# Activation tiles moved by 64 bytes, the convolution's tap blocks on VectorE, and a new order of its steps

## The chip, the cores and the metric

The kernel runs on one core of a Trainium2 chip. The metric is the device time of one execution in microseconds (us), as the median of several runs. Engines are named as the profile names them: PE (TensorE's matmuls), PEld (TensorE's weight loads), DVE (VectorE), ACT (ScalarE), POOL (GpSimd) and SP (SyncE, which issues DMAs).

## The reference

The input is 256 positions of 1,024 channels in float32. Two transformer layers and a third block follow one another; each needs the result of the one before.

```python
def first_block(...):
    for layer in range(2):
        mix = even_mixer(...) if layer % 2 == 0 else odd_mixer(...)
        h = h + mix
        h = h + swiglu(rmsnorm(h, g_ffn[layer]), w_gate[layer], w_up[layer], w_down[layer])
        gate = sigmoid(rmsnorm(h, g_ple[layer]) @ w_ple_gate[layer])
        h = h + gate * (p[layer] @ w_ple_proj[layer])

def conformer_conv(h, w_in, b_in, w_dw, b_dw, ln_g, ln_b, w_out):
    a, gt = split(h @ w_in + b_in)
    u = a * sigmoid(gt)
    y = depthwise_causal_conv31(u, w_dw) + b_dw
    return silu(layernorm(y, ln_g, ln_b)) @ w_out

def second_block(x, c, ...):
    x = x + g1 * conformer_conv(rmsnorm_2(x, g) * (1 + sc1) + sh1, ...)
    x = x + g2 * hier_moe(rmsnorm_2(x, g) * (1 + sc2) + sh2, ...)
    return rmsnorm_2(x, final_g)
```

The mixers are a short gated convolution with spatial gating (layer 0) and an attention with a chunked recurrence (layer 1). `hier_moe` sends each position to 2 of 32 experts. The change acts on all the dense products and on `conformer_conv`, whose depthwise convolution has 31 taps.

## The kernel before, in words

**Dense products.** A weight comes from HBM in pieces of 128x2048 into `raw` (`load`, line 153, issued by SP). `prep` (line 160) splits a piece into two tiles of the type fp32r in one slot `hl`: ACT copies the high part (line 66 is the helper that records it), DVE subtracts it to get the low part (line 70). Activations are split in the same way: `xTh` and `xTl` hold the transposed input, high and low; `aTh`/`aTl`, `yTh`/`yTl` and others hold those of other products. A product is three matmuls (`mm3`, line 118, or `passes`, line 1286), high by high, high by low and low by high, all recorded at line 111. In nearly all of them the activation is the stationary operand (128x128, loaded by PEld) and the weights stream past it, 512 columns at a time. In the convolution's input product (the steps named i below) it is the other way round: `hl` is stationary and 256 columns of `xTh` or `xTl` stream.

**Addresses.** `shift_by(pool, n)` (line 34) allocates a gap of n bytes per partition, so that all tiles behind it in the pool move. Before, the gap ahead of `xTh` is 64 bytes. In the built program `xTh` then stands at byte 12192 of each partition, which is 160 modulo 256, and so do `xTl` and the other split activations; each slot of `hl` is 224 modulo 256. The activations stand 64 bytes below the weights, modulo 256.

**The conformer convolution.** The 1,024 channels are eight tiles m = 0 to 7 of 128. The first three tiles' input products are made for each half h of the positions, with the activations stationary, the others by `conv_in_proj(m)`, 48 matmuls of 256 columns each. `conv_u(m)` (line 1180) makes the gated tile u: ACT takes the tanh, DVE multiplies (line 79). Tile 0 is convolved on DVE, tap by tap (`yc<-u,wtap,yc`, line 79, one 128x256 instruction for a tap), drained in the background while PE goes on. Tiles 1 to 7 are convolved on PE: POOL's queue writes u to `ud` in HBM (line 1197), the closure `back` has SP read it again in another layout, four DMAs into `u4` (line 1202, three buffers), and `conv_pe(m)` (line 1262) runs 64 matmuls of 256 columns (line 1266) whose stationary operands are the tap blocks `taps[m]`. A tap block is a 128x1024 product of the filter `wcv` with the identity, made by `conv_taps_w(m)` (line 1174), on POOL before (`e=G`); there are four buffers (`TAPS`), so the block of tile m+4 is made behind `conv_pe(m)`. The first four are issued ahead of the products of tiles 0 to 2 (line 1289).

**The order.** The program is scheduled by hand: instructions run on each engine in the order in which the code issues them, and DMAs queue on SP in the same way. The loop at line 1426 follows a string, `TG["plan"]` (line 1919): iM is `conv_in_proj(M)`, cM is `conv_pe(M)`, r issues the reads waiting in `reads` except the last, a issues all of them, s is `conv_pivot` (a mean over two tiles that the other tiles are shifted by), R and t prepare the router's weights (`r_start`, line 1333, begins with an iota on POOL and three small DVE operations), p preps a weight of the next product. Each matmul counted by `mm` may also release background work.

**After it** come the layer norm, the output product, the router, and the experts' stage, in which weights of 1 MB each are read from HBM, in fp32 and used once.

Of the kernel before, what the change touches and what calls it, by code (L numbers as in the profile page):

```python
# [11 lines left out]
I32 = mybir.dt.int32  # L12
# [11 lines left out]
FAR = 1024.0  # L24
# [9 lines left out]
def shift_by(pool, n):  # L34

    gaps.append(n)
    pool.tile([128, n // 4], F32, name=f"gap{len(gaps)}", tag=f"gap{len(gaps)}")
# [3 lines left out]
def kernel(ctx, tc, A, out, stop=None):  # L41
    nc = tc.nc
    V, S, T, G, SP = nc.vector, nc.scalar, nc.tensor, nc.gpsimd, nc.sync
# [7 lines left out]
    xp = ctx.enter_context(tc.tile_pool(name="xp", bufs=1))  # L51
# [3 lines left out]
    dconst = dense_stack.enter_context(tc.tile_pool(name="dconst", bufs=1, side="right"))  # L55
    small = dense_stack.enter_context(tc.tile_pool(name="small", bufs=2, side="right", reuse_waits="tile"))
# [7 lines left out]
    def act(o, i, f, scale=1.0, bias=0.0, accum_out=None):  # L64
        if accum_out is None:
            return S.activation(o, i, f, bias=bias, scale=scale)  # L66
        return S.activation(o, i, f, bias=bias, scale=scale, accum_out=accum_out)  # L67

    def tt(o, a, b, op, e=None):
        return (e or V).tensor_tensor(o, a, b, op=op)  # L70

    def ts(o, a, s1, s2, op0, op1=None, e=None):
        if op1 is None:
            return (e or V).tensor_scalar(o, a, s1, None, op0=op0)  # L74
        return (e or V).tensor_scalar(o, a, s1, s2, op0=op0, op1=op1)
# [6 lines left out]
    def red(o, i, op):  # L82
        return V.tensor_reduce(o, i, op=op, axis=AX.X)

    MUL, ADD, SUB, MAX, MIN = ALU.mult, ALU.add, ALU.subtract, ALU.max, ALU.min
# [101 lines left out]
    def nxt(kept=False):  # L187
        i = at_[1]
        at_[1] += 1
        if kept:  # L190
            hold.append(first_half[i])
        return lambda k: need(i, k)


    X = xp.tile([128, 2, D], F32, name="X")
    shift_by(xp, 64)
    xTh = xp.tile([128, 2, 8, 128], F32R, name="xTh", tag="xTh")
    xTl = xp.tile([128, 2, 8, 128], F32R, name="xTl", tag="xTl")

# [5 lines left out]
                    base=0, channel_multiplier=-1)  # L205
# [7 lines left out]
                    base=0, channel_multiplier=-1)  # L213
# [3 lines left out]
                    base=0, channel_multiplier=-1)  # L217
    ones = const.tile([128, 128], F32, name="ones")
    G.memset(ones, 1.0)

    col, ncol = col_plan()
    vc = dconst.tile([128, ncol], F32, name="vc")
# [883 lines left out]
    eye = dconst.tile([128, 32], F32, name="eye")  # L1106
# [13 lines left out]
    def preload(n):  # L1120
        while len(moe_w) < min(n, 6 * NEXP):
            q = len(moe_w)
            pair, r = divmod(q, 12)
            s_ = q % SLOTS
            if s_ < EARLY:
                t_ = early.tile([128, 2048], F32, name="ew", tag="ew")
            elif s_ < EARLY + NEXT:
                t_ = nexts.tile([128, 2048], F32, name="nw", tag="nw")
            elif s_ < EARLY + NEXT + RING:
                t_ = ring.tile([128, 2048], F32, name="raw", tag="raw")  # L1130
            elif s_ < EARLY + NEXT + RING + WRING:
                t_ = wring.tile([128, 2048], F32, name="wr", tag="wr")
            else:
                t_ = split.tile([128, 2048], F32, name="hl", tag="hl")
            if q < 6 * NEXP - 2:
                SP.dma_start(t_, A["moe"][2 * pair + r % 2, r // 2])
            moe_w.append(t_)
            if q == 6 * NEXP - 1:
                for c in range(2):
                    for e in range(2):  # L1140
                        sl = slice(1024 * c, 1024 * c + 1024)
                        SP.dma_start(moe_w[q - 1 + e][:, sl], A["moe"][2 * pair + e, 5, :, sl])
# [9 lines left out]
    iota64 = rt.tile([128, 64], F32, name="iota64")  # L1152
    iom = rt.tile([128, 32], F32, name="iom")
# [2 lines left out]
    gate = rt.tile([128, 2, 32], F32, name="gate")  # L1156
    rank = rt.tile([128, 2, 32], F32, name="rank")
    cnt = rt.tile([128, 32], F32, name="cnt")
    cstk = ExitStack()
    cp = cstk.enter_context(tc.tile_pool(name="conv", bufs=1, side="right", reuse_waits="tile"))  # L1160
    ustk = ExitStack()
# [10 lines left out]
    taps, u4, reads = {}, {}, []  # L1172

    def conv_taps_w(m):

        taps[m] = cu.tile([128, 32, 32], F32, name="taps", tag="taps", bufs=TAPS)
        tt(taps[m], wsh[:, m, :, None].to_broadcast([128, 32, 32]),
           eye[:, None, :].to_broadcast([128, 32, 32]), MUL, e=G)

    def conv_u(m, pt):  # L1180
        sg = cu.tile([128, 256], F32, name="sg", tag="sg", bufs=2)
# [80 lines left out]
    def conv_pe(m):  # L1262
        pt = psum("mm")
        for i in range(8):
            for g in range(4):
                T.matmul(pt[32 * g:32 * g + 32, 0:256], taps[m][:, 8 * g + i, :],
                         u4[m][:, g, 4 * i:4 * i + 256], start=i == 0, stop=i == 7)
            if background:
                background.pop(0)[1]()
        if m in PIVOT:  # L1270
            act(yc[:, m, :], pt[:, 0:256], AF.Identity, bias=vc[:, c0 + m:c0 + m + 1])
        else:
            stt(yc[:, m, :], pt[:, 0:256], vc[:, c0 + m:c0 + m + 1], shift, ADD, SUB)
            conv_sums(m)

    def conv_pivot():

        pt = psum("aux")
        for m in PIVOT:
            T.matmul(pt[:, 0:256], ones, yc[:, m, :], start=m == PIVOT[0], stop=m == PIVOT[-1])  # L1280
        ts(shift, pt[:, 0:256], 1.0 / 256, None, MUL)
        shifted[0] = True
        for m in list(PIVOT) + unshifted:
            conv_shift(m)
# [1 line left out]
    def passes(wk):  # L1286
        return ((wk[0], xTh), (wk[0], xTl), (wk[1], xTh))

    for m in range(ONDVE, ONDVE + TAPS):
        conv_taps_w(m)  # L1290
    first_w = [nxt(True) for _ in range(3)]
    pm = [psum("mm") for _ in range(3)]
    um, us = {}, {}
# [22 lines left out]
    def conv_in_proj(m):  # L1316
        w = nxt(True)
        pt = psum("mm")
        for c in range(2):
            o = pt[:, 256 * c:256 * c + 256].rearrange("p (h t) -> p h t", h=2)  # L1320
            for k in range(8):
                for i, (w_, x_) in enumerate(passes(w(k))):
                    mm(o, w_[:, c * 128:(c + 1) * 128], x_[:, :, k, :], k == 0 and i == 0, k == 7 and i == 2)
        hold.clear()
        conv_u(m, pt)
# [4 lines left out]
    def rtile(name, *shape, pool=None):  # L1330
        return (pool or rt).tile([128] + list(shape), F32, name=name)

    def r_start():

        iota_i = small.tile([128, 512], I32, name="iota_i", tag="xf")[:, 0:64]
        G.iota(iota_i, pattern=[[1, 64]], base=0, channel_multiplier=0)
        V.tensor_copy(iota64, iota_i)
        ts(iom, iota64[:, 0:32], -64.0, None, ADD)
        ts(iota64, iota64, -FAR, None, ADD)
        wr = vc[:, col["w_r"]:col["w_r"] + 288].rearrange("p (k n) -> p k n", k=8)  # L1340
        gs = small.tile([128, 512], F32, name="gs", tag="xf")[:, 0:288].rearrange("p (k n) -> p k n", k=8)
        tt(gs, wr, modc[:, 24:32, None].to_broadcast([128, 8, 36]), MUL)
        shw = rtile("shw", 36, pool=cp)
        red(shw, gs.rearrange("p k n -> p n k"), ADD)
        gw = wr
        tt(gw, wr, moe_g[:, :, None].to_broadcast([128, 8, 36]), MUL)
        router.extend([gw, shw])

    def r_shift():
        pt = psum("aux")  # L1350
        T.matmul(pt[:, 0:36], ones, router[1], start=True, stop=True)
        rc = rtile("rc", 36, pool=cp)
        tt(rc, pt[:, 0:36], row("b_r"), ADD)
        router[1] = rc
# [60 lines left out]
    def r_rank():  # L1415
# [6 lines left out]
        stt(rank, asg, -FAR, rp[:, 0:64].rearrange("p (h e) -> p h e", h=2), MUL, ADD)  # L1422
        act(cnt, rp[:, 64:96], AF.Copy)

    bg_every[0] = TG["bg"][1]
    for step in TG["plan"].split():
        m = int(step[1:] or 0)
        if step[0] == "i":
            conv_in_proj(m)
        elif step in "ra":  # L1430
            while len(reads) > (step == "r"):
                reads.pop(0)()
        elif step == "o":
            preload(len(moe_w) + 1)
        elif step[0] == "c":
            conv_pe(m)
            if m + TAPS < 8:
                conv_taps_w(m + TAPS)
        elif step == "s":
            conv_pivot()  # L1440
        elif step == "R":
            r_start()
        elif step == "t":
            r_shift()
        elif step == "p" and at_[0] < len(halves):
            prep()
# [403 lines left out]
    R, frow = end[2], end[1]  # L1850
# [32 lines left out]
def bass_f32(x, bits=24):  # L1883
# [7 lines left out]
ONDVE = 1  # L1891
LN_AHEAD = 5
TAPS = 4
# [26 lines left out]
}  # L1920
PIVOT = (1, 2)
K8 = ((0, 4), (4, 4))
# [58 lines left out]
def col_plan():  # L1981
    return offsets(COLS, lambda o, n: o)
# [74 lines left out]
```

## Time and profile before

| what | value |
|---|---|
| median of 3 runs | 1265.97 us (1257.66 to 1267.45) |
| the profiled execution: its time, and its span | 1260.12 us, 1258.3 us |
| PE busy | 1191.8 us, 95% of the span |
| PEld busy | 817.2 us, 65% |
| DVE, ACT, POOL busy | 647.2 us (51%), 482.9 us (38%), 76.3 us (6%) |
| moved by DMA | 361.87 MB, mean 288 GB/s |
| mean granted TensorE clock | 0.992 |

The span is the stretch of the profiled execution that the trace covers; 1.8 us of that execution's time lie around it. A busy PE is not PE at its peak, since matmuls are pipelined and their recorded lengths overlap; the distance from one start to the next, called the pitch here, says what a matmul costs in a row of them. A granted clock of 1.00 is 2.4 GHz, 0.50 is 1.2 GHz.

### The profile page before, as it was taken

How to read it: one execution, taken by the hardware profiler on the slowest of the kernel's cores; microseconds unless marked ns; L12 is line 12 of the kernel's file. 1: busy time of each engine (PE TensorE's matmuls, PEld its weight loads, DVE VectorE, ACT ScalarE, POOL GpSimd, SP SyncE). 2: the span in 40 equal slices, each digit the busy share in tenths (PEclk: the TensorE clock that was granted, in tenths of full speed). 3: DMA queues.
4: the chain of work that ended last, by engine and by line, in shares of the span. 5: the costliest groups of instructions: out<-in, count | busy, mean ns of one | idle time of the engine just before them, and what ended most of it. 6: DMA issues, size and time to landing. Idle time of an engine off the chain costs nothing. (4 is left out here: it accounts for less than half of the span.)

```text
span 1258.3 us, 15805 instructions
## 1 busy us (share of the span) xinstructions
PE 1191.8 (95%) x6143; PEld 817.2 (65%) x6143; DVE 647.2 (51%) x1079; ACT 482.9 (38%) x802; POOL 76.3 (6%) x109
## 2 busy tenths in 40 slices
PE   7999999999889999999998899999999999898995
PEld 5888888888777788888887777444444444343432
DVE  6767677677767688775465865522112221111114
ACT  7545544446875474444364433311101111110111
POOL 1100000001030000000004140000000000000000
PEclk9999999999999999999999999999999999999999
DMA  9654777874533189765644759699999999999992
GB/s 332 237 168 184 263 279 269 285 300 140 183 136 130 38 325 374 270 236 196 216 135 182 228 182 393 259 421 421 420 420 421 420 421 419 422 420 421 421 419 100
DMA packets 60716, 361.87 MB, mean 288 GB/s; under 512 B 7296, under 2 KB 11040, under 8 KB 22496
## 3 DMA queue, kind: packets, MB, share of 16 engines
q1 hardware_dynamic: 59184, 357.27, 73.5%
q0 software_dynamic: 1024, 3.05, 0.8%
q8 instruction: 49, 0.80, 0.3%
q10 hardware_dynamic: 432, 0.53, 0.1%
q14 instruction: 27, 0.22, 0.1%
HBM read 358.71 MB, written 2.11 MB: 287 GB/s over the span
## 5 line engine op out<-in xcount | busy, mean ns | idle before, releaser
L111 PE MATMUL mm<-hl,xTh 128*128 128x512 f32 (+3 forms) x1376 | 423.9, 388 | 12.4 <-ACT hl L66 6.0
L70 DVE TENSOR_TENSOR hl<-raw,hl 128x1024 fp32r<-128x1024 f32 (+3 forms) x240 | 284.7, 1217 | 94.0 <-ACT hl L66 90.6
L111 PEld LDWEIGHTS mm<-hl,xTh 128*128 128x128 f32 x1376 | 256.0, 190 | 64.2 <-ACT hl L66 6.4
L66 ACT ACTIVATE hl<-raw 128x1024 fp32r<-128x1024 f32 (+3 forms) x240 | 240.7, 1032 | 136.9 <-PE mm L111 102.1
L111 PE MATMUL mm<-hl,xTl 128*128 128x512 f32 (+3 forms) x688 | 265.5, 386 | 2.7 <-DVE xTl L70 2.7
L111 PEld LDWEIGHTS mm<-hl,xTl 128*128 128x128 f32 x688 | 130.7, 190 | 28.2 <-DVE xTl L70 3.8
L111 PE MATMUL mm<-hl,aTh 128*128 128x512 f32 x352 | 109.7, 392 | 0.0
L1625 PE MATMUL gu<-hl,xg 128*64 128x512 f32 x392 | 101.6, 603 | 5.9 <-DMA hl<-in_moe_dram 5.9
L70 DVE TENSOR_TENSOR hid<-gu,hid 128x512 f32<-128x512 f32 x16 | 11.1, 692 | 184.4 <-PE gu L1625 184.4
L1625 PEld LDWEIGHTS gu<-hl,xg 128*64 128x64 f32 x392 | 35.3, 139 | 62.4 <-issue 51.2
L111 PEld LDWEIGHTS mm<-hl,aTh 128*128 128x128 f32 x352 | 66.1, 188 | 13.8
L79 DVE SCALAR_TENSOR_TENSOR yhl<-w,gc,yhl 128x512 fp32r<-128x512 f32 x30 | 22.5, 751 | 97.3 <-ACT yhl L66 95.4
L111 PE MATMUL mm<-hl,aTl 128*128 128x512 f32 x176 | 69.3, 394 | 0.0
L1625 PE MATMUL gu<-wr,xg 128*64 128x512 f32 x216 | 63.1, 595 | 5.5 <-DMA wr<-in_moe_dram 5.5
L80 DVE SCALAR_TENSOR_TENSOR ada<-ada,crow 128x1024 f32<-128x1024 f32 x48 | 58.4, 1220 | 7.3 <-DMA ada<-in_ada_dram 7.3
L66 ACT ACTIVATE yhl<-w,gc 128x512 fp32r<-128x512 f32 x30 | 20.6, 687 | 106.1 <-PE w L1650 106.1
L66 ACT ACTIVATE xg<-w,modc,moe_g 128x256 f32<-128x256 f32 x32 | 18.1, 564 | 85.3 <-PE w L1596 85.3
L1650 PE MATMUL w<-hl,hid 128*64 128x512 f32 x184 | 47.6, 597 | 3.3 <-DVE ogT L74 3.3
L66 ACT ACTIVATE hid<-gu 128x512 f32<-128x512 f32 x16 | 9.6, 597 | 102.0 <-PE gu L1625 102.0
L1625 PE MATMUL gu<-raw,xg 128*64 128x512 f32 x152 | 44.5, 593 | 0.9 <-DMA raw<-in_moe_dram 0.9
L1625 PE MATMUL gu<-ew,xg 128*64 128x512 f32 x152 | 43.7, 594 | 0.4 <-DMA ew<-in_moe_dram 0.4
L1625 PEld LDWEIGHTS gu<-wr,xg 128*64 128x64 f32 x216 | 20.6, 137 | 36.1 <-issue 25.1
(453 smaller groups left out, 1494.8 us busy)
## 6 DMA issues: line engine op xcount, KB each, us to landing
raw<-in_dense_dram SPq DMA_DIRECT2D x108, 1024.0 KB, 5.2
hl<-in_moe_dram SPq DMA_DIRECT2D x72, 1024.0 KB, 19.8
wr<-in_moe_dram SPq DMA_DIRECT2D x45, 1024.0 KB, 19.8
ew<-in_moe_dram SPq DMA_DIRECT2D x28, 1024.0 KB, 19.9
raw<-in_moe_dram SPq DMA_DIRECT2D x27, 1024.0 KB, 19.8
ada<-in_ada_dram SPq DMA_DIRECT2D x48, 512.0 KB, 7.7
nw<-in_moe_dram SPq DMA_DIRECT2D x18, 1024.0 KB, 19.8
raw<-in_dense_dram SPq DMA_DIRECT2D x8, 512.0 KB, 6.9
```

Source lines behind the costliest of these rows:

```text
L66: return S.activation(o, i, f, bias=bias, scale=scale)
L70: return (e or V).tensor_tensor(o, a, b, op=op)
L79: return V.scalar_tensor_tensor(o, a, s, b, op0=op0, op1=op1)
L80: return V.scalar_tensor_tensor(o, a, s, b, op0=op0, op1=op1, accum_out=accum_out)
L111: T.matmul(o, lhsT, rhs, start=start, stop=stop_)
L1625: T.matmul(o[64 * e:64 * e + 64, :], xg[:, k, s0 + 64 * e:s0 + 64 * e + 64], ws[e][:, kk * 512:(kk + 1) * 512], start=k == 0, stop=k == 7)
L1650: T.matmul(py[c][64 * e:64 * e + 64, :], hT[:, k, 64 * e:64 * e + 64], ws[e][:, (2 * c + kk) * 512:(2 * c + kk + 1) * 512], start=k == 0, ...
```

## The change

It has four parts. (1) The gap ahead of `xTh` grows from 64 to 128 bytes: `xTh` stands at byte 12256, 224 modulo 256, like the slots of `hl`, and the other split activations move with it to the same residue. (2) DVE makes the tap blocks instead of POOL, and the first four are issued behind the products of tiles 0 to 2, ahead of the plan. (3) The plan changes: each r now issues exactly one read, and the steps c come later among the steps i. (4) The router's iota moves to the start of the kernel, and its three small DVE operations ahead of the convolution.

```diff
-    shift_by(xp, 64)
+    shift_by(xp, 128)
...
+    iota_i = dconst.tile([128, 64], I32, name="iota_i")
+    G.iota(iota_i, pattern=[[1, 64]], base=0, channel_multiplier=0)
...
+    V.tensor_copy(iota64, iota_i)
+    ts(iom, iota64[:, 0:32], -64.0, None, ADD)
+    ts(iota64, iota64, -FAR, None, ADD)
...
         taps[m] = cu.tile([128, 32, 32], F32, name="taps", tag="taps", bufs=TAPS)
         tt(taps[m], wsh[:, m, :, None].to_broadcast([128, 32, 32]),
-           eye[:, None, :].to_broadcast([128, 32, 32]), MUL, e=G)
+           eye[:, None, :].to_broadcast([128, 32, 32]), MUL)
...
-    for m in range(ONDVE, ONDVE + TAPS):
-        conv_taps_w(m)
     first_w = [nxt(True) for _ in range(3)]
...
-        iota_i = small.tile([128, 512], I32, name="iota_i", tag="xf")[:, 0:64]
-        G.iota(iota_i, pattern=[[1, 64]], base=0, channel_multiplier=0)
-        V.tensor_copy(iota64, iota_i)
-        ts(iom, iota64[:, 0:32], -64.0, None, ADD)
-        ts(iota64, iota64, -FAR, None, ADD)
...
+    for m in range(ONDVE, ONDVE + TAPS):
+        conv_taps_w(m)
     bg_every[0] = TG["bg"][1]
     for step in TG["plan"].split():
         m = int(step[1:] or 0)
         if step[0] == "i":
             conv_in_proj(m)
-        elif step in "ra":
-            while len(reads) > (step == "r"):
-                reads.pop(0)()
+        elif step[0] == "r":
+            reads.pop(0)()
...
-    "plan": "i3 r i4 r c1 R i5 r c2 s i6 t r c3 i7 r c4 p p p c5 a c6 c7",
+    "plan": "i3 r1 r2 i4 r3 R i5 c1 i6 r4 t c2 s i7 r5 c3 p p p r6 c4 r7 c5 c6 c7",
```

On DVE, in the program before, the instructions from the split of the convolution's input (second half of the positions) to the third gated tile stand so (`hl<-raw,hl` is the low part of a weight, `u<-sg,u` the end of a gated tile u):

```order
L283 CAST xTh<-xf 128x512
L70 TENSOR_TENSOR xTl<-xf,xTh 128x512
L79 SCALAR_TENSOR_TENSOR u_5574<-sg,u_5574 128x256
L75 TENSOR_SCALAR yc<-u_5574,wtap,vc 128x256
L79 SCALAR_TENSOR_TENSOR yc<-u_5574,wtap,yc 128x256
L79 SCALAR_TENSOR_TENSOR u<-sg,u 128x256
L79 SCALAR_TENSOR_TENSOR yc<-u_5574,wtap,yc 128x256 x2
L70 TENSOR_TENSOR hl<-raw,hl 128x1024 x4
L79 SCALAR_TENSOR_TENSOR yc<-u_5574,wtap,yc 128x256
L79 SCALAR_TENSOR_TENSOR u<-sg,u 128x256
L70 TENSOR_TENSOR hl<-raw,hl 128x1024 x2
```

The same stretch of DVE's queue in the changed program:

```order
L285 CAST xTh<-xf 128x512
L70 TENSOR_TENSOR xTl<-xf,xTh 128x512
L79 SCALAR_TENSOR_TENSOR u_5571<-sg,u_5571 128x256
L75 TENSOR_SCALAR yc<-u_5571,wtap,vc 128x256
L79 SCALAR_TENSOR_TENSOR yc<-u_5571,wtap,yc 128x256
L79 SCALAR_TENSOR_TENSOR u<-sg,u 128x256
L79 SCALAR_TENSOR_TENSOR yc<-u_5571,wtap,yc 128x256 x2
L70 TENSOR_TENSOR taps<-wcv,eye 128x1024 x4
L70 TENSOR_TENSOR hl<-raw,hl 128x1024 x4
L79 SCALAR_TENSOR_TENSOR yc<-u_5571,wtap,yc 128x256
L79 SCALAR_TENSOR_TENSOR u<-sg,u 128x256
L70 TENSOR_TENSOR hl<-raw,hl 128x1024 x2
```

Four tap blocks now stand ahead of the low parts of the next weights; the rest of the stretch is as it was.

On SP, in the program before, the weight loads (`raw<-in_dense_dram`) and the reads of `ud` into `u4` (shown as `u_`, in the order of the tiles 1 to 7) stand so from the convolution's last weights on:

```order
L153 DMA raw<-in_dense_dram 128x2048 x5
L1202 DMA u_5736<-ud 32x4x284 x4
L1202 DMA u_5741<-ud 32x4x284 x4
L153 DMA raw<-in_dense_dram 128x2048
L1202 DMA u_5817<-ud 32x4x284 x4
L153 DMA raw<-in_dense_dram 128x2048
L1202 DMA u_5947<-ud 32x4x284 x4
L153 DMA raw<-in_dense_dram 128x2048
L1202 DMA u_6080<-ud 32x4x284 x4
L1202 DMA u_6188<-ud 32x4x284 x4
L1202 DMA u_6273<-ud 32x4x284 x4
L1136 DMA raw<-in_moe_dram 128x2048 x3
```

The same stretch of SP's queue in the changed program:

```order
L153 DMA raw<-in_dense_dram 128x2048 x5
L1207 DMA u_5741<-ud 32x4x284 x4
L1207 DMA u_5746<-ud 32x4x284 x4
L153 DMA raw<-in_dense_dram 128x2048
L1207 DMA u_5822<-ud 32x4x284 x4
L153 DMA raw<-in_dense_dram 128x2048 x2
L1207 DMA u_6018<-ud 32x4x284 x4
L1207 DMA u_6144<-ud 32x4x284 x4
L1207 DMA u_6194<-ud 32x4x284 x4
L1207 DMA u_6236<-ud 32x4x284 x4
L1138 DMA raw<-in_moe_dram 128x2048 x3
```

The first two reads keep their place behind the same five weight loads; the fourth now stands behind one weight load more. On PE the order of the steps was i3 i4 c1 i5 c2 s i6 t c3 i7 c4 c5 c6 c7 and is now i3 i4 i5 c1 i6 t c2 s i7 c3 c4 c5 c6 c7.

## Rows read from the trace of the kernel before

**Rows 1.** L111's two largest forms by shape: busy us, mean ns; idle before by releaser
```profile
L111 PE MATMUL mm<-hl,xTh 128*128 128x512 f32 x1216 | 389.5, 399 | 8.3 <-ACT hl L66 6.0 <-DVE hl L70 1.2 <-ACT xTh L66 1.0
L111 PE MATMUL mm<-hl,xTl 128*128 128x512 f32 x608 | 240.4, 395 | 0.2 <-DVE xTl L70 0.2
```

**Rows 2.** PE on the timeline, 200 to 206 us: start us, length us, instruction
```profile
200.34 0.39 PE L111 MATMUL mm<-hl,xTl 128*128 128x512 f32 x1
...
205.84 0.39 PE L111 MATMUL mm<-hl,xTl 128*128 128x512 f32 x1
```

**Rows 3.** windows: span; busy us of PE, PEld, DVE, ACT, POOL; clock, DMA share, GB/s
```profile
780.00:800.00 20.00, 18.83 (x118) 13.46 (x118) 13.02 (x44) 7.62 (x16) 1.66 (x6) 1.00 0.57 218
820.00:1000.00 180.00, 177.74 (x876) 82.84 (x872) 36.96 (x84) 26.09 (x43) 0.00 (x0) 1.00 1.01 420
```

**Rows 4.** PE on the timeline, 680 to 740 us; in brackets the wait and its releaser
```profile
680.40 0.39 PE L111 MATMUL mm<-hl,xTh 128*128 128x256 f32 x1 [2.76 <-DVE xTh L283]
682.71 0.58 PE L111 MATMUL mm<-hl,xTl 128*128 128x256 f32 x1 [1.93 <-DVE xTl L70]
...
704.90 0.28 PE L111 MATMUL mm<-xTh,hl 128*128 128x256 f32 x1
709.09 5.35 PE L1266 MATMUL mm<-u,taps 128*32 128x256 f32 x64 [3.91 <-DMA u<-ud]
...
720.22 3.66 PE L1266 MATMUL mm<-u,taps 128*32 128x256 f32 x64
```

**Rows 5.** VectorE on the timeline, 665 to 700 us
```profile
665.95 0.43 DVE L283 CAST xTh<-xf 128x512 fp32r<-128x512 f32 x1 [4.14 <-ACT xf L66]
666.48 0.69 DVE L70 TENSOR_TENSOR xTl<-xf,xTh 128x512 fp32r<-128x512 f32 x1
...
678.32 2.02 DVE L283 CAST xTh<-xf 128x512 fp32r<-128x512 f32 x1 [1.90 <-ACT xf L66]
680.38 2.28 DVE L70 TENSOR_TENSOR xTl<-xf,xTh 128x512 fp32r<-128x512 f32 x1
...
693.42 1.00 DVE L79 SCALAR_TENSOR_TENSOR yc<-u,wtap,yc 128x256 f32<-128x256 f32 x2
695.28 4.63 DVE L70 TENSOR_TENSOR hl<-raw,hl 128x1024 fp32r<-128x1024 f32 x4 [0.86 <-ACT hl L66]
```

**Rows 6.** GpSimd on the timeline, 675 to 685 us
```profile
675.70 8.72 POOL L70 TENSOR_TENSOR taps<-wcv,eye 128x1024 f32<-128x1024 f32 x4 [1.15 <-DMA wcv<-in_w_conv_dram]
```

**Rows 7.** windows of the two slow stretches, columns as in rows 3
```profile
682.60:686.00 3.40, 3.29 (x14) 3.15 (x15) 2.80 (x3) 0.00 (x0) 2.21 (x4) 0.50 0.00 0
709.10:714.40 5.30, 5.30 (x65) 3.29 (x65) 4.34 (x10) 0.00 (x0) 0.54 (x1) 0.68 0.97 287
```

**Rows 8.** SyncE's queue on the timeline, 690 to 720 us
```profile
700.36 9.33 SPq L1202 DMA_DIRECT2D u<-ud  x8
```

**Rows 9.** PE, 256-column matmuls at 668, 696 and 715 us
```profile
668.04 0.28 PE L111 MATMUL mm<-hl,xTl 128*128 128x256 f32 x1
...
675.46 0.28 PE L111 MATMUL mm<-hl,xTl 128*128 128x256 f32 x1
...
695.95 0.28 PE L111 MATMUL mm<-xTl,hl 128*128 128x256 f32 x1
...
704.79 0.28 PE L111 MATMUL mm<-xTl,hl 128*128 128x256 f32 x1
...
715.29 0.28 PE L111 MATMUL mm<-xTl,hl 128*128 128x256 f32 x1
...
717.06 0.28 PE L111 MATMUL mm<-xTl,hl 128*128 128x256 f32 x1
```

**Rows 10.** PE, gathering matmuls of the expert stage
```profile
802.73 0.28 PE L1596 MATMUL w<-oh,xTl 128*128 128x256 f32 x1
...
804.17 0.28 PE L1596 MATMUL w<-oh,xTl 128*128 128x256 f32 x1
```

**Rows 11.** PE, bf16 filler matmuls at 759 us
```profile
759.45 1.90 PE L128 MATMUL aux<-ones_b 128*128 128x512 bf16 x8
```

## The prediction

> **What bounds the kernel now.** I read the page's shares first: PE is busy for 95% of the span, every other engine for half of it or much less. That is an average over stages, so I then took the groups by shape, and the stages one by one.
>
> In the dense part, up to about 690 us, PE is the bound. The two largest groups hold 1,824 matmuls of 512 columns and hardly any idle time in front of them [rows 1]; with the smaller groups of 512 columns in the same view (those of `aTh`, `aTl`, `yTh`, `yTl`, `pTh`, `pTl`, `kvh` and `kvl`) it is 2,520. Their mean lengths of 395 to 399 ns overlap and are no price. The price is the pitch: from 200.34 to 205.84 us, 24 matmuls follow without a gap, 5.50 us / 24 = 229 ns each [rows 2].
>
> In the experts' stage the weights' transfer is the bound: from 820 to 1000 us DMA is busy all the time and moves 420 GB/s, with PE busy beside it [rows 3]. From 780 to 800 us it moves only 218 GB/s, because the loads that run ahead have filled their buffers and wait for the experts to begin. So a start that comes earlier by some time should bring the end forward by as much: what is gained before they begin passes to the end at full price. The experts themselves are not sped up by anything here.
>
> Between them lies the convolution, and there PE waits. The reader is to see three places on the timeline [rows 4]: the first matmul of the second half waits 2.76 us for DVE's `xTh`, the first with `xTl` waits 1.93 us for DVE again, and c1 waits 3.91 us for its read of `ud`. After c1, PE runs without such waits to the end of c7.
>
> **The change part by part.** *A, the tap blocks leave POOL.* On DVE the cast that makes `xTh` takes 0.43 us and the subtraction that makes `xTl` 0.69 us at 666 us, but 2.02 and 2.28 us at 678 and 680 us [rows 5]. All that lies beside them is POOL's four tap blocks, 675.70 to 684.42 us, 8.72 / 4 = 2.18 us each [rows 6]. Without them I take the short durations: the cast ends at 678.32 + 0.43 = 678.75, the subtraction about 0.05 + 0.69 later at 679.5, and the matmul that starts at 682.71 can start there: 3.2 us. Behind that wait the granted clock is 0.50 from 682.6 to 686.0, with 14 matmuls in 3.40 us [rows 7]; at full clock they need 14 x 0.118 = 1.65 us (pitch below). PE would stand idle for about 1.9 us there instead of 4.7 in two pieces, so I let the clock stay up: 1.75 us more. A = 4.9 us, 3.2 if it falls all the same.
>
> *B, c1 moves behind i5.* c1's predecessor starts at 704.90 and c1 at 709.09, so 4.07 us are lost, and c1 itself takes 5.35 us where the same 64 matmuls take 3.66 us later [rows 4], with a clock of 0.68 over it [rows 7]: 1.7 us. Together 5.8 us. But the read does not come as early as PE will. SP issues it at 700.36 [rows 8], right behind a weight load that waits for DVE's fourth low part, which ends at 695.28 + 4.63 = 699.91 [rows 5]; the data comes 8.7 us after the issue. With A, DVE is free at 694.42 - 4.9 = 689.5 instead of 694.42; four tap blocks and four low parts of 1.16 us each (below) end at 698.8, so the read is issued 1.1 us earlier and lands at 708.0. PE ends i4 4.9 us earlier and C (below) later, at 700.5, and then does i5, 48 x 0.118 = 5.65 us: c1 is due at about 706.2. A wait of 1.7 us remains. B = 5.8 - 1.7 = 4.1 us; 5.8 if the read is faster with less traffic ahead, 1.9 if the wait is longer by half a microsecond and the clock drops again.
>
> *C, four tap blocks ahead of i4's low parts.* No row shows a tap block on DVE. The nearest is the low part, the same 128x1024 with two inputs from SBUF: 4.63 / 4 = 1.16 us [rows 5]. The bounds are that and POOL's 2.18 us [rows 6]; I take 1.16 because it is the same engine and operation. The first low part for i4 is then ready at 689.5 + 4.64 + 1.16 = 695.3, and i4's third matmul wants it at about 694.9: a stall of 0.4 us. In the program before, DVE waits 0.86 us for ACT in that place [rows 5], which covers part. At POOL's price it is 4.1 us more.
>
> *D, the later blocks, the later reads, the iota.* Three more blocks on DVE, 3.5 us spread over c1 to c3, and the fourth read behind one weight load more on SP. What follows the last tile is u7, its write, its read (8.7 us, as above), c7. Between i7 and c7 the new order has c3 to c6 on PE, 4 x 3.66 = 14.6 us [rows 4] and some small matmuls, which cover u7's DVE work, the write and the read with a few us left. I take 0, and up to 2 us if they don't. The iota goes to POOL's idle start, and its three DVE operations of 128x64 or less stand where DVE waits for ACT (4.14 us at 665.95, [rows 5]): 0.
>
> *E, the addresses.* Nothing in the trace shows 512 columns with stationary and moving at one residue, and a change of 1 ns in the pitch is worth 2.5 us. Nearest rows: with the stationary 64 bytes below, 668.04 to 675.46 us is 63 matmuls of 256 columns at 117.8 ns; with it 64 bytes above, 695.95 to 704.79 is 78 at 113.3, but 715.29 to 717.06 is 15 at 118 [rows 9]. At one residue, 802.73 to 804.17 is 12 at 120.0 [rows 10]. So the residue alone does not set the pitch: the same one shows two levels. Bounds: 120.0 - 117.8 = +2.2 ns for 256 columns, +4.4 for 512, times 2,520 = +11 us; downwards the quickest 512 columns of the trace, the fillers, 8 in 1.90 us: with 0.39 us for the last of them, as long as a single one in rows 2, the seven pitches are 1.51 / 7 = 216 ns [rows 11], 13 ns less, -33 us. I take 0, nearest to the rows without a change of level: 118 and 120 against 117.8 is no step that I can tell from none.
>
> The Trainium skill, "TensorE: Matmul & The Clock Gate", Part 2, step 1 (LDWEIGHTS), says that the stationary and the moving operand have read ports of their own and loading one takes no bandwidth from the other; by that E is 0 at any residue. Two levels at one residue [rows 9] neither need nor exclude it.
>
> The sum: 4.9 + 4.1 - 0.4 = 8.6 us. The profiled execution goes from 1260.1 to 1251.5 us. It lies 5.9 us under the median of the runs, 1266.0; from there I forecast 1257.4 us.
>
> **The rivals.** *The pitch falls.* If the 64 bytes cost something in each matmul now, the dense part gets it back. For it: 229 ns against 216 for fillers whose stationary and moving operand are one small tile [rows 2, 11], and no DMA or wait that would explain 229. Against it: rows 10. At -4.5 ns, the difference of 117.8 and 113.3, it is -11 us, so 1246; at the floor -33, so 1224. The same page, "Back-to-back issue gap", gives about 216 ns for 512 columns; were all of the excess due to residues, an estimate from that figure is 13 x 2.52 = 33 us.
>
> *The pitch rises,* the one that ends on the other side: one residue makes weight load and stream meet in the same place of the memory. For it: 120.0 [rows 10], the longest of the 256-column pitches. Against it: 118 to 120 is little. At +4.4 ns it costs 11.1 us, which leaves 1257.4 + 11.1 = 1268.5 us, slower than before. It decides from 8.6 / 2.52 = 3.4 ns on, a pitch of 232.4; slower by over 1% (12.7 us) needs 8.4 ns.
>
> *DVE becomes the convolution's bound:* tap blocks at 2.18 us, i4 stalled by 4.5 us instead of 0.4, and the chain to c7 by up to 2. Against it: the row of the low part. Time: 8.6 - 4.1 - 2 = 2.5 us gained, 1263.5.
>
> *B comes to nothing,* since the read waits for SP as before: B = 1.9 or less, 1260; this lies in the forecast's own range.
>
> **How the numbers follow.** Forecast 0.43 (its own range 1252 to 1264: the ends of A, B and C, and 1 ns of pitch), a falling pitch 0.33, a rising one 0.15, DVE as the bound 0.09. A third of the falling case (0.11) lies below 1238 us, which needs 7.7 ns; half of the rising one (0.08) lies above 1268: the range is 1238 to 1268 us. Faster by over 1%, about what a measurement of this kernel can tell from no change, needs 1253.3: 0.31 of the falling case and 0.04 of the forecast. Slower by over 1%, above 1278.6, is half of the rising case, 0.07. Within 1%: 0.58.
>
> **What would show it.** A: the cast and subtraction of the second half at 0.43 and 0.69 us, no clock of 0.50 behind them. B: c1 behind i5 with a wait under 2 us, then 3.66 us. C: tap blocks at 1.16 us on DVE and a stall of under 1 us in i4. D: c7 without a wait, and the experts' stage starting some 8.6 us earlier, at 420 GB/s as before. E: a pitch of 229 ns between 200 and 206 us; if it is anything else, the forecast is wrong by 2.5 us for each ns, and that is its weakest term.

## The result and the profile after

| | median of its runs | ratio to the kernel before |
|---|---|---|
| before | 1266.22 us (1257.66 to 1267.45, 4 runs) | |
| changed | 1250.93 us (1247.28 to 1251.20, 4 runs) | 0.9887, interval 0.984 to 0.9934 |
| changed, later, on one chip with more runs of before | 1251.22 us (6 runs), before 1264.32 us (23 runs) | 0.9911, interval 0.9883 to 0.9939 |

The change makes the kernel about 1% faster; the two intervals reach from 0.6% to 1.6%. A ratio is estimated from all runs of both kernels and is not the quotient of the two medians beside it. The forecast was 1257.4 us, 8.6 us less than before; the time lies in the range of 1238 to 1268 us. The profiled executions differ by 1260.12 - 1250.80 = 9.3 us, less than the medians do; the last experiment shows one source of such scatter.

The changed kernel's timeline of PE (start, length, instruction; in brackets the wait and its releaser), to be held against [rows 4] and [rows 9]:

```profile
676.03 0.38 PE L111 MATMUL mm<-hl,xTh 128*128 128x256 f32 x1 [1.16 <-DVE xTh L285]
676.75 0.39 PE L111 MATMUL mm<-hl,xTl 128*128 128x256 f32 x1 [0.34 <-DVE xTl L70]
...
693.05 0.28 PE L111 MATMUL mm<-xTl,hl 128*128 128x256 f32 x1
...
703.84 0.28 PE L111 MATMUL mm<-xTl,hl 128*128 128x256 f32 x1
...
705.50 3.66 PE L1271 MATMUL mm<-u,taps 128*32 128x256 f32 x64 [1.26 <-DMA u<-ud]
...
745.91 0.61 PE L1223 MATMUL tp<-per_d,yc 128*128 128x1 f32 x4 [0.61 <-DVE yc L79]
```

Of the three waits, the first (2.76 us) is 1.16 now, the second (1.93) is 0.34, and c1, behind i5, waits 1.26 us for its read where it waited 3.91; it then takes 3.66 us and not 5.35. The two `xTl` matmuls at 693.05 and 703.84 are 90 matmuls of 256 columns apart: 119.9 ns each, against 113.3 to 118 in [rows 9]. The last row is the first small matmul behind c7.

VectorE's timeline of the changed kernel, which answers to [rows 5]:

```profile
675.55 0.43 DVE L285 CAST xTh<-xf 128x512 fp32r<-128x512 f32 x1 [2.04 <-ACT xf L66]
676.01 0.69 DVE L70 TENSOR_TENSOR xTl<-xf,xTh 128x512 fp32r<-128x512 f32 x1
...
686.89 4.63 DVE L70 TENSOR_TENSOR taps<-wcv,eye 128x1024 f32<-128x1024 f32 x4
691.44 4.62 DVE L70 TENSOR_TENSOR hl<-raw,hl 128x1024 fp32r<-128x1024 f32 x4
...
724.34 1.30 DVE L70 TENSOR_TENSOR yc<-yc,shift 128x256 f32<-128x256 f32 x3
...
732.96 3.00 DVE L70 TENSOR_TENSOR hl<-raw,hl 128x1024 fp32r<-128x1024 f32 x2 [0.36 <-ACT hl L66]
```

Cast and subtraction are back at 0.43 and 0.69 us. Four tap blocks take 4.63 us on DVE, 1.16 each, like the low parts behind them. POOL's 8.72 us [rows 6] are gone.

Windows of the changed kernel: the stretch behind the two matmuls of the second half, c1, and the middle of the experts' stage, with the columns of [rows 3]:

```profile
676.50:680.00 3.50, 3.25 (x27) 3.25 (x28) 1.32 (x3) 0.59 (x3) 0.00 (x0) 1.00 0.65 257
705.40:709.30 3.90, 3.80 (x65) 2.60 (x66) 3.87 (x8) 1.96 (x5) 0.71 (x3) 1.00 0.95 261
820.00:1000.00 180.00, 177.54 (x879) 84.00 (x877) 37.50 (x85) 26.92 (x44) 0.00 (x0) 1.00 1.01 420
```

The granted clock is 1.00 in the first two stretches, 0.50 and 0.68 before [rows 7]. The experts still run at 420 GB/s. SyncE's queue, for [rows 8]:

```profile
696.51 9.34 SPq L1207 DMA_DIRECT2D u<-ud  x8
```

The reads for c1 and c2 are issued 3.85 us earlier than before (700.36); the data lands at 705.5.

PE's timeline of the changed kernel at the place of [rows 2]:

```profile
200.25 0.39 PE L111 MATMUL mm<-hl,xTl 128*128 128x512 f32 x1
...
205.69 0.39 PE L111 MATMUL mm<-hl,xTl 128*128 128x512 f32 x1
```

24 matmuls in 5.44 us: 226.7 ns, where they took 229.2. PE's first matmul with `xTl` behind the dense part, in the kernel before and in the changed one:

```profile
667.23 0.38 PE L111 MATMUL mm<-hl,xTl 128*128 128x256 f32 x1 [0.41 <-DVE xTl L70]
```

```profile
664.32 0.39 PE L111 MATMUL mm<-hl,xTl 128*128 128x256 f32 x1 [0.41 <-DVE xTl L70]
```

It comes 2.9 us earlier. The stretch's 2.5 ns times 2,520 matmuls would be 6.3 us, so the stretch does not stand for all: over all stretches without a gap in the two traces the mean pitch is 229.0 ns before and 227.2 now, 1.8 ns less.

The two ends of the convolution in the kernel before, not shown so far (the first small matmul behind c7, and the experts' first):

```profile
756.99 0.61 PE L1218 MATMUL tp<-per_d,yc 128*128 128x1 f32 x4 [0.61 <-DVE yc L79]
...
796.16 0.36 PE L1596 MATMUL w<-oh,xTh 128*128 128x256 f32 x1
```

and the experts' first in the changed kernel:

```profile
784.92 0.36 PE L1595 MATMUL w<-oh,xTh 128*128 128x256 f32 x1
```

So c7 is done 756.99 - 745.91 = 11.1 us earlier, and the experts begin 796.16 - 784.92 = 11.2 us earlier.

### The profile page after: what moved, and what is told of

The parts are those of the page before. It is cut to its first block, busy times and chain, and to the rows that moved or that the text cites. A ratio compares the mean times of both kernels' runs of the same rounds, so it can differ in the third digit from the quotient of the medians.

```text
span 1249.1 us, 15809 instructions
## 1 busy us (share of the span) xinstructions
PE 1188.5 (95%) x6143; PEld 818.9 (66%) x6143; DVE 646.2 (52%) x1086; ACT 482.4 (39%) x802; POOL 62.7 (5%) x102
## 5 line engine op out<-in xcount | busy, mean ns | idle before, releaser
L111 PE MATMUL mm<-hl,xTh 128*128 128x512 f32 (+3 forms) x1376 | 419.7, 385 | 10.9 <-ACT hl L66 6.6
L111 PEld LDWEIGHTS mm<-hl,xTh 128*128 128x128 f32 x1376 | 255.0, 189 | 60.9 <-ACT hl L66 7.0
L111 PE MATMUL mm<-hl,xTl 128*128 128x512 f32 (+3 forms) x688 | 264.8, 385 | 1.1 <-DVE xTl L70 1.1
L111 PEld LDWEIGHTS mm<-hl,xTl 128*128 128x128 f32 x688 | 130.2, 189 | 24.9 <-DVE xTl L70 2.2
L111 PE MATMUL mm<-hl,aTh 128*128 128x512 f32 x352 | 109.0, 390 | 0.0
L70 DVE TENSOR_TENSOR hid<-gu,hid 128x512 f32<-128x512 f32 x16 | 11.1, 691 | 185.2 <-PE gu L1624 185.2
L111 PEld LDWEIGHTS mm<-hl,aTh 128*128 128x128 f32 x352 | 66.1, 188 | 13.7
L111 PE MATMUL mm<-hl,aTl 128*128 128x512 f32 x176 | 68.9, 391 | 0.0
```

The costliest lines, as they stand in the source:

```text
L111: T.matmul(o, lhsT, rhs, start=start, stop=stop_)
```

## The experiments

The experiments take the change apart. Part (4), the router's iota, was run with the others only; in the kernel before it takes POOL 0.18 us (at 716.42), so it can explain little of the result. Four kernels were run first on one chip, each with part of the change, against 29 runs of the kernel before (median 1262.79 us).

**The addresses alone** (e1_addr), in the kernel before:

```diff
-    shift_by(xp, 64)
+    shift_by(xp, 128)
```

> The kernel before with the 128-byte gap alone (one residue for split activations and weights). Theory: the dense products' pitch falls from 229 to about 227.5 ns per 512 columns, the first convolution matmul with xTl comes about 3 us earlier, and the whole is 3 to 4 us faster (ratio 0.997). c1's wait of about 4 us and the slow stretch behind the tap blocks stay. Rival 1, the addresses do nothing and the 3 us by which the dense part ended earlier in the changed kernel are scatter of one execution: ratio 1.000, pitch 229. Rival 2, the addresses carry most of the result: ratio 0.990 or less.

Measured: 1260.71 us, ratio 0.9982 (0.9966 to 0.9999). PE's timeline of this kernel:

```profile
200.30 0.39 PE L111 MATMUL mm<-hl,xTl 128*128 128x512 f32 x1
...
205.74 0.39 PE L111 MATMUL mm<-hl,xTl 128*128 128x512 f32 x1
...
678.19 0.58 PE L111 MATMUL mm<-hl,xTl 128*128 128x256 f32 x1 [1.93 <-DVE xTl L70]
...
704.80 5.35 PE L1266 MATMUL mm<-u,taps 128*32 128x256 f32 x64 [3.46 <-DMA u<-ud]
```

The pitch is 5.44 / 24 = 226.7 ns, and the matmul with `xTl` comes at 678.19 instead of 682.71, with its wait as before; c1 still waits 3.46 us. So the addresses do something by themselves, though less than the 3 to 4 us expected: the trace has c1 some 4 us earlier, and 2.1 us show in the median.

**All parts but the addresses** (e2_no_addr), the changed kernel with `shift_by(xp, 64)`:

> The changed kernel with the 64-byte gap of before (all parts but the addresses). Theory: pitch back at 229 ns, the dense part ends 3 to 4 us later than in the changed kernel, the convolution keeps its gain of about 8 us: ratio 0.9935, some 8 us faster than before. Rival 1, the addresses do nothing: the same ratio as the changed kernel, 0.989. Rival 2, addresses carry most: ratio 0.998 or above.

Measured: 1256.06 us, ratio 0.9935 (0.9919 to 0.9951), as the theory had it.

```profile
708.30 3.66 PE L1271 MATMUL mm<-u,taps 128*32 128x256 f32 x64 [1.31 <-DMA u<-ud]
```

c1 waits 1.31 us, as in the changed kernel. Addresses (0.9982) and the rest (0.9935) multiply to 0.9917; the whole measured 0.9911.

**The tap blocks on DVE, old plan** (e3_taps_dve), in the kernel before:

```diff
-           eye[:, None, :].to_broadcast([128, 32, 32]), MUL, e=G)
+           eye[:, None, :].to_broadcast([128, 32, 32]), MUL)
...
-    for m in range(ONDVE, ONDVE + TAPS):
-        conv_taps_w(m)
     first_w = [nxt(True) for _ in range(3)]
...
+    for m in range(ONDVE, ONDVE + TAPS):
+        conv_taps_w(m)
     bg_every[0] = TG["bg"][1]
```

> The kernel before with the tap blocks on DVE behind the first three tiles, under the old plan. Theory: the cast and subtraction of the second half return to 0.43 and 0.69 us and PE reaches the convolution 4.7 us earlier, but c1 still stands behind i4 and waits for its read, which is issued only about 1 us earlier: PE's wait at c1 grows from 3.9 to 7 or 8 us and the kernel gains 1 us at most (ratio 0.999 to 1.000). Rival, the two parts of the gain add up: 4.7 us faster, ratio 0.996, c1's wait unchanged at about 4 us.

Measured: 1261.15 us, ratio 0.9983 (0.9965 to 1.000). PE's timeline, then SyncE's queue:

```profile
680.50 0.38 PE L111 MATMUL mm<-hl,xTl 128*128 128x256 f32 x1 [0.34 <-DVE xTl L70]
...
710.37 4.96 PE L1266 MATMUL mm<-u,taps 128*32 128x256 f32 x64 [8.54 <-DMA u<-ud]
```

```profile
700.14 9.99 SPq L1202 DMA_DIRECT2D u<-ud  x8
```

PE arrives earlier and waits it off: c1 starts at 710.37, after a wait of 8.54 us. The read is issued at 700.14 where it was 700.36 (the first `xTl` behind the dense part stands at 668.20 here and at 667.23 there, so the read gained about 1.2 us on PE), since the weight load ahead of it on SP is released by DVE's low parts and the four tap blocks now stand ahead of those. The mend of one wait is eaten by the next.

**The new plan alone, tap blocks on POOL** (e4_plan), in the kernel before:

```diff
-        elif step in "ra":
-            while len(reads) > (step == "r"):
-                reads.pop(0)()
+        elif step[0] == "r":
+            reads.pop(0)()
...
-    "plan": "i3 r i4 r c1 R i5 r c2 s i6 t r c3 i7 r c4 p p p c5 a c6 c7",
+    "plan": "i3 r1 r2 i4 r3 R i5 c1 i6 r4 t c2 s i7 r5 c3 p p p r6 c4 r7 c5 c6 c7",
```

> The kernel before with the new plan alone, tap blocks on POOL as before. Theory: c1 stands behind i5 and finds its read landed, 4.1 us of wait and 1.7 us of slow clock gone: 5.8 us faster (ratio 0.9955), while the waits for DVE of 2.76 and 1.93 us and the clock of 0.50 behind them stay. With the tap blocks on POOL the read is not delayed by them, so this part alone brings more than its share in the changed kernel (3.7 us). Rival, the plan alone brings nothing since the read is late as before: ratio 1.000, c1 waiting about 4 us.

Measured: 1265.19 us, ratio 0.9999 (0.998 to 1.0019). The expectation missed the total, not its first step. PE's timeline:

```profile
710.01 3.66 PE L1266 MATMUL mm<-u,taps 128*32 128x256 f32 x64
...
747.19 0.61 PE L1218 MATMUL tp<-per_d,squares 128*128 128x1 f32 x4 [3.23 <-POOL squares L70]
...
750.52 5.68 PE L1266 MATMUL mm<-u,taps 128*32 128x256 f32 x64
```

c1 has no wait and no slow clock any more, as expected. But the small matmuls ahead of c7 wait 3.23 us for POOL's running sums, and c7 behind them takes 5.68 instead of 3.66 us; the first small matmul behind c7 starts at 756.82, where it was 756.99. VectorE's and GpSimd's timelines of this kernel show why the sums are late:

```profile
728.82 3.42 DVE L70 TENSOR_TENSOR yc<-yc,shift 128x256 f32<-128x256 f32 x3
...
739.71 4.80 DVE L70 TENSOR_TENSOR hl<-raw,hl 128x1024 fp32r<-128x1024 f32 x2 [1.49 <-ACT hl L66]
```

```profile
740.38 1.91 POOL L70 TENSOR_TENSOR taps<-wcv,eye 128x1024 f32<-128x1024 f32 x1
...
747.09 0.73 POOL L70 TENSOR_TENSOR squares<-squares 128x256 f32<-128x256 f32 x1
```

Three subtractions of 128x256 take 3.42 us and two low parts 4.80; in the changed kernel the same ones take 1.30 and 3.00 (724.34 and 732.96 above). While they run, POOL makes tap blocks (at 729.48 and 740.38) and adds up the sums. DVE's slow low parts hold up `yc`, on which the next sums wait, and the last sum begins at 747.09. So the new plan needs the tap blocks off POOL, as those need the new plan: alone 0.0% and -0.2%, together (with part 4, in e2_no_addr) -0.65%.

The next four ran together against 23 runs of before. **The changed kernel again** (e5_after) is the third row of the result's table.

> The changed kernel, measured on the same chip as the next three. Theory: the four parts run alone gave -0.2% (addresses), -0.2% (tap blocks), 0.0% (plan) and, tap blocks with plan, -0.65%; with the addresses the whole should be -0.85 to -1.0%: ratio 0.990 to 0.9915. Rival, the first comparison's 0.9887 holds and there is more than these parts: 0.987 to 0.989.

Measured: 0.9911 (0.9883 to 0.9939); the expected 0.990 to 0.9915 lies within the interval, and so does the upper end of the rival's range, so the rival is not excluded.

**Other distances**: the changed kernel with `shift_by(xp, 192)` (e6_shift192) and `shift_by(xp, 256)` (e7_shift256).

> The changed kernel with a gap of 192 bytes: the split activations stand 64 bytes above the weights modulo 256. Theory, one residue is the best place for 512 columns: the pitch goes back to 229 ns and the dense part ends 3 to 4 us later than in the changed kernel, while the products with 256 streaming columns take 116 to 118 ns instead of 120; ratio 0.992 to 0.994. Rival, what counted is the distance from 64 bytes below, and any other place is as good: pitch 227.4 ns, ratio as the changed kernel's.

> The changed kernel with a gap of 256 bytes: the split activations stand 128 bytes away from the weights modulo 256. Theory, one residue is the best place for 512 columns: pitch 229 ns or more, ratio 0.992 to 0.994. Rival, the farther the better: pitch 226 ns or less and a ratio below the changed kernel's.

Measured: 1264.83 us, ratio 1.0008 (0.9991 to 1.0026), and 1258.58 us, 0.9967 (0.995 to 0.9983). PE's timelines of e6_shift192 and of e7_shift256:

```profile
200.00 0.39 PE L111 MATMUL mm<-hl,xTl 128*128 128x512 f32 x1
...
205.60 0.39 PE L111 MATMUL mm<-hl,xTl 128*128 128x512 f32 x1
```

```profile
200.29 0.40 PE L111 MATMUL mm<-hl,xTl 128*128 128x512 f32 x1
...
205.89 0.40 PE L111 MATMUL mm<-hl,xTl 128*128 128x512 f32 x1
```

Both have 5.60 / 24 = 233.3 ns. Both expectations had the direction, but their ratios (0.992 to 0.994) were too low, and the 229 ns of the first too. One residue is the best of the places tried, and both other places cost more than 64 bytes below did: 13.6 us and 7.4 us against the changed kernel's median, for the same pitch in this stretch. Up to the end of the dense part the two traces agree within 0.6 us (table below); why 6 us lie between their medians stays open. With 64 bytes above, all that the rest of the change gains is lost.

**32 bytes to either side** (e9_shift96, e10_shift160), in the version with the reordered tail (below, 1246.77 us, 0.9871), with gaps of 96 and 160 bytes:

> The version with the reordered tail and a gap of 96 bytes: split activations 32 bytes below the weights modulo 256. Theory, the pitch rises with the distance from one residue: between 227.4 and 229.1 ns, 0 to 4 us slower than the same version at one residue (ratio 0.987 to 0.990). Rival, one residue is no optimum and the best lies between: pitch under 227 ns, ratio under 0.986.

> The version with the reordered tail and a gap of 160 bytes: split activations 32 bytes above the weights modulo 256. Theory, the pitch rises with the distance from one residue, and faster on this side (233.3 ns at 64 bytes above): 229 to 231 ns, 4 to 9 us slower than the same version at one residue (ratio 0.990 to 0.994). Rival, one residue is no optimum and the best lies between: pitch under 227 ns, ratio under 0.986.

Measured: 1257.49 us, 0.9936 (0.9912 to 0.9959), and 1255.61 us, 0.9921 (0.9897 to 0.9944). PE's timelines of e9_shift96 and of e10_shift160:

```profile
200.06 0.40 PE L111 MATMUL mm<-hl,xTl 128*128 128x512 f32 x1
...
205.66 0.40 PE L111 MATMUL mm<-hl,xTl 128*128 128x512 f32 x1
```

```profile
200.03 0.40 PE L111 MATMUL mm<-hl,xTl 128*128 128x512 f32 x1
...
205.63 0.40 PE L111 MATMUL mm<-hl,xTl 128*128 128x512 f32 x1
```

The expectation of an orderly rise fell: at 32 bytes on either side the same 24 matmuls take 5.60 us, no less than at 64 above.

**The weights moved instead** (e11_both64): the gap is 64 again, and a gap of 64 bytes ahead of the weights' slots moves those (and the rest of that side) to 160 modulo 256.

```diff
-    shift_by(xp, 128)
+    shift_by(xp, 64)
...
+    shift_by(ctx.enter_context(tc.tile_pool(name="above", bufs=1, side="right")), 64)
     split = ctx.enter_context(tc.tile_pool(name="split", bufs=SPLIT, side="right"))
```

> The version with the reordered tail, the gap of 64 bytes of the kernel before, and the weights' slots (with all else at that end of the memory) moved down by 64 bytes as well: activations and weights both at 160 modulo 256. Theory, only the distance between the two counts: pitch 227.4 ns, the time of the reordered version (ratio 0.986 to 0.989). Rival, the place of the activations itself counts: pitch 229.1 ns as in the kernel before, or 233, and 3 to 15 us slower than the reordered version (ratio 0.990 to 0.999).

Measured: 1246.78 us, ratio 0.9885 (0.985 to 0.9921) against six runs of before with a median of 1261.22 us; the reordered version's own median is 1246.77 us.

```profile
200.52 0.39 PE L112 MATMUL mm<-hl,xTl 128*128 128x512 f32 x1
...
205.96 0.39 PE L112 MATMUL mm<-hl,xTl 128*128 128x512 f32 x1
```

5.44 us again. At distance 0 the place made no difference: the distance counts, as far as these two places show. The table collects the 24 matmuls between 200 and 206 us and the start of the first matmul with `xTl` behind the dense part, over all traces with that distance (the last column varies by over 2 us between executions at one distance, so single pairs of it are to be read with care):

| activations stand | 24 matmuls of 512 columns | each | first `xTl` behind the dense part |
|---|---|---|---|
| at the weights' residue (changed, e1, e5, e8, e11) | 5.44 us | 226.7 ns | 662.7 to 665.4 us |
| 64 bytes below (before, e2, e3, e4) | 5.50 us | 229.2 ns | 665.9 to 668.2 us |
| 32 below, 32 above, 64 above, 128 away (e9, e10, e6, e7) | 5.60 us | 233.3 ns | 674.9 to 676.3 us |

The gap moves `raw`, which lies right behind `xTl`, along with the activations in every one of these programs. So no run separates the distance between PE's two operands from that between `raw` and the weights' slots. The pitch differs also in the output product, where ACT and DVE are busy for 0.73 and 2.17 us of 6 (769 to 775 us in the kernel before): 228.9 ns before (from 768.22 to 780.58 us, 54 matmuls) and 226.7 ns now (from 755.06 to 769.34 us, 63 matmuls). That speaks for PE's operands; it is not a proof.

**The tail** (e8_tail), in the changed kernel. `gather_up(h)` adds the running sum of half h to X on DVE, four instructions; the edit puts that of the second half behind `gc` and `ogT`, which free a PSUM bank that PE wants for the last pair of experts:

```diff
                 combine2(j, prev[0], i == 1, final)
-                if final:
-                    gather_up(j)
+                if final and j == 0:
+                    gather_up(0)
...
                 backs[i] = way_back(onehots[i], 128)
+                if final:
+                    gather_up(1)
```

> The changed kernel with one edit in the last pair of experts: DVE makes gc and ogT for the last pair ahead of the second half of the running sum (gather_up(1)) instead of behind it. Theory: PE's wait of 3.24 us for DVE ogT ahead of the last down product shrinks to under 1 us, the clock no longer falls behind it in some executions, and the kernel is 2.4 to 5 us faster than the changed one (ratio to the kernel before 0.985 to 0.988). Rival, the wait moves to DVE's later work (its adds then stand ahead of the last gated products) or to the 2.14 us wait that follows: no gain over the changed kernel.

Measured: 1246.77 us (1246.03 to 1247.30), ratio 0.9871 (0.9847 to 0.9895), with e11_both64 the fastest of the study. The same matmul of the last pair in three traces, first the changed kernel's profiled execution, then that of e5_after (the same program), each with the next one of its kind:

```profile
1227.85 0.61 PE L1649 MATMUL w<-hl,hid 128*64 128x512 f32 x1 [3.24 <-DVE ogT L74]
...
1228.30 0.59 PE L1649 MATMUL w<-hl,hid 128*64 128x512 f32 x1
```

```profile
1225.49 1.09 PE L1649 MATMUL w<-hl,hid 128*64 128x512 f32 x1 [3.23 <-DVE ogT L74]
...
1226.37 1.06 PE L1649 MATMUL w<-hl,hid 128*64 128x512 f32 x1
```

In both PE waits 3.2 us. Behind the wait the first keeps its clock: from 1227.85 to 1228.30, 0.45 us, and a clock of 1.00. In the second the same step takes 0.88 us, at a clock of 0.62. The windows behind the wait, first the changed kernel's, then that of e5_after:

```profile
1227.80:1232.80 5.00, 4.95 (x22) 1.72 (x22) 0.40 (x1) 0.00 (x0) 0.00 (x0) 1.00 0.00 0
```

```profile
1225.40:1233.30 7.90, 7.80 (x22) 2.32 (x22) 0.35 (x1) 0.00 (x0) 0.00 (x0) 0.62 0.00 0
```

PE's timeline of e8_tail, and DVE's order there:

```profile
1224.33 0.61 PE L1649 MATMUL w<-hl,hid 128*64 128x512 f32 x1 [0.57 <-DVE ogT L74]
```

```profile
1223.44 0.42 DVE L83 TENSOR_REDUCE gc<-w 128x1 f32<-128x256 f32 x1
1223.77 0.42 DVE L74 TENSOR_SCALAR ogT<-w 128x256 fp32r<-128x256 f32 x1
1224.10 0.68 DVE L70 TENSOR_TENSOR raw<-acc,raw 128x512 f32<-128x512 f32 x1
```

The wait is 0.57 us, 2.7 us less than in either trace of the changed kernel; the slow clock behind it, which one of those two has and the other not, did not show in e8_tail's profile. Its five runs lie within 1.3 us, those of e5_after within 7.9 us; the three versions with the same tail and other addresses (e9 to e11) have 2.6 to 4.6 us. So the wait is one source of the scatter and not the only one: in e9_shift96 the clock falls to 0.66 between 1220 and 1230 us, at an earlier pair.

## Why the prediction was right, and where it was not

The direction, the range and most steps held; the size was 8.6 us forecast against 11.1 us at the end of c7. Of the 2.5 us between them the addresses (E) account for 2.0 and B with C for 0.8, while A fell short by 0.3.

- *What bounds, and the full price of an earlier start.* Right: 11.1 us at c7, 11.2 us at the experts' first matmul. Of the profiled pair 1.9 us are lost again behind that, by the clock among the last pairs of experts (0.94 and 0.71 in the two stretches of 10 us from 1200 to 1220 us in the changed kernel, where the kernel before has 0.83 from 1220 to 1230: 0.6 + 2.9 - 1.7 = 1.8 us); the ratio over more runs, 0.9911 of 1264.3 us, is 11.3 us.
- *A,* 4.9 us. The second wait's matmul comes 5.96 us earlier, of which the dense part has brought about 2.9 (the first half's matmul with `xTl` comes at 664.32 instead of 667.23 us); 3.1 are left, 3.2 were forecast. The clock behind it stays at 1.00, as taken; the start of the first transposes of u, 688.30 before and 680.81 now, adds 1.5 us where 1.75 were forecast. A was 4.6. The idle time that the prediction left in the two waits, 1.9 us, does not follow from its own terms, which leave 4.7 - 3.2 = 1.5; measured are 1.16 + 0.34 = 1.50. The sum did not use it.
- *B,* 4.1 us with a remaining wait of 1.7. The wait is 1.26, since the read was issued at 696.51; the clock did not fall. e4_plan shows the move of c1 behind i5 by itself, and e3_taps_dve what the tap blocks do without it: a wait of 8.54 us.
- *C,* a stall of 0.4 us. A tap block costs the 1.16 us taken from the low part. In i4 one step of three matmuls takes 0.50 us (692.55 to 693.05) instead of 0.36, a stall of 0.14; in e2_no_addr it is 0.80 (695.19 to 695.99) instead of 0.34, a stall of 0.46. B and C together gave 0.8 us more than forecast, taken as what the other terms leave of the 11.1.
- *D,* nothing. Right for the changed kernel, in part by luck: the prediction followed u7's read, while the chain that is nearly too late is that of POOL's running sums. With the tap blocks on POOL (e4_plan) the small matmuls ahead of c7 wait 3.23 us for it; in the changed kernel the last sum ends at 739.31 and they start at 739.76.
- *E,* nothing. This is the term that failed. The pitch fell by 2.5 ns in the stretch of [rows 2], and the dense part ended about 3 us earlier in the profiled pair (2.9 at the place above, with the scatter that the table shows); alone it measured 0.9982. The step that failed is the reading of [rows 9, 10]: 120.0 ns at one residue was taken as no step, and carried to 512 columns. It is a step, since all input products of the convolution with 256 columns take 120 ns now, about 0.9 us more over the 240 of i3 to i7 (their mean distance is 116.1 ns before and 119.9 now); but 512 columns go the other way. The forecast's own range (1252 to 1264) was left by about 1 us; what happened is the forecast's case with a small piece of the rival of a falling pitch.
- *The rival that the pitch rises* was one choice of residue away: at 64 bytes above it is 233.3 ns and the whole gain is gone, with the break-even stated at 232.4.
- *DVE as the bound* did not come: 1.16 us a block.

The sum at c7: A 4.6, B and C the remaining 4.5 (3.7 forecast), addresses 2.9 in the dense part and -0.9 in the 256 columns: 11.1 us.

The Trainium skill, "TensorE: Matmul & The Clock Gate", Part 2, step 1, has loading and streaming on ports of their own; by that the distance between the two operands would not count. The rows above differ with it by 6.6 ns in 226.7, so the measurement decides: the distance counts, with the reservation on `raw` made above. Why it does stays open, and nothing here shows it.

## What to carry to other kernels

Mend waits in one stage together and look for what is late next: two edits that each brought a fifth of a per cent or nothing brought 0.65% at once (with part 4), because each removed the wait that the other ran into. Where PE streams hundreds of large matmuls in a row, try the address of the stationary operand against the streaming one as a parameter of its own, measured at the column count that carries the time. And look at what stands on another engine ahead of an operation that frees a buffer for PE: 0.8 us of work that waited behind 2.7 us of other work cost PE those 2.7 us in the traces, and the medians differ by 4.5.

## What was not expected of the hardware

A difference of 32 bytes in where two tiles stand modulo 256 costs 233.3 - 226.7 = 6.6 ns in each matmul of 512 columns of the stretch, 9 to 11 us of this kernel (1255.61 and 1257.49 against 1246.77), and the smallest of the distances tried is no cheaper than the largest. At 256 columns one residue is the slowest place instead: 119.9 ns, against about 113 to 119 at the other distances. And the same program can keep its clock behind a PE wait of 3.24 us in one execution and lose it in the next (1.00 and 0.62), which makes part of the scatter between runs; without the wait the runs lay within 1.3 to 4.6 us instead of 7.9.
